# A hybrid decoder block on one core: transposing moves from GpSimd's queue, a double block of gate and z, and a third seven-product pair in every second gate and up block

## The chip, the cores and the metric

One core of a Trainium2 chip runs the whole kernel. The metric is the device time of one execution in microseconds; lower is better.

## What is computed

The reference is one layer of a decoder (256 tokens, model width 2048, all float32), and this is its skeleton:

```python
h = rmsnorm(x, ln1_w)
q, k, v, u, z, xbc, dt_raw, gate_logits = split(h @ w_in)
att  = sink_window_attention(q, k, v, sink)
pool = multiscale_pool(u, pool_w, pool_scale)
ssm  = ssd_mixer(z, xbc, dt_raw, ...)     # y * silu(z), normed in 4 groups of 512
g = sigmoid(gate_logits)                  # 3 x 2048 columns
merged = g[0]*(att @ w_attn_br) + g[1]*(pool @ w_pool_br) + g[2]*(ssm @ w_ssm_br)
x = x + merged @ w_out
h2 = rmsnorm(x, ln2_w)
gate, up = split(h2 @ w_gate_up)          # 2 x 5632 columns
x = x + (silu(gate) * up) @ w_down
out = rmsnorm(x, final_w)
```

## The kernel before

**Products in three.** Each float32 operand is split into a rounded part `hi` (a ScalarE copy, line 142) and the rest `lo` (a VectorE subtraction, line 143). A product is three matmuls, hi·hi, hi·lo and lo·hi (lines 225 to 227, function `three`). The activations stand transposed in SBUF, 128 of the inner dimension per tile ("k tile"); weights stream from HBM through the SyncE (SP) queue. `weights` loads into `raw` (3 buffers) and splits into two pieces of 128x1024, `whi` and `wlo`, of which there are 5 buffers each. So VectorE and ScalarE prepare weights at most five pieces ahead of TensorE.

**Blocks.** `tokens_block` makes 512 output columns for both token tiles. `two_blocks` makes 2 x 512 columns and takes the k tiles in pairs. A plain pair costs 8 products of 128x512 (24 matmuls, two weight pieces). A "seven" pair is a 2x2 by 2x2 block product by the Strassen and Winograd scheme: 7 products (21 matmuls). It needs sums of weights, made on VectorE from the tile `sraw` (1 buffer) and `vu` (1 buffer) in `block_weights` (lines 290 to 313: three splits of 128x1024, one addition of 128x1024, two additions of 128x512, one split of 128x512 into `shi`, `slo`), and sums of activations, made once in `block_forms` (tile `forms`). In a block of 8 pairs, pairs 0 and 1 are seven pairs and the order is 0, 2, 3, 4, 1, 5, 6, 7. Four of the eight accumulators (`tr`, `sm` in PSUM) end with the last seven pair and are folded into others by VectorE (lines 360 to 364).

**Turning.** A block of results [tokens x 512 columns] that becomes the next matmul's operand is transposed by `turn`: `move` issues 16 DMAs of 32x(2x128) blocks from SBUF to the tile `mid` (line 497), then `parts` transposes 32x32 squares on VectorE (line 502) and splits. There are four such turns for the SSD output (`ssm`, after each z group), four for the merged sum (`mp`), four for the residual (`x2p`) and eleven for the feed-forward (`f`). Before the change the `mp` moves go through GpSimd's (POOL) queue, all others through SP's queue, between the weight loads.

**Order.** `later` puts such side work in a list of tasks with a cost; `side`, called after each weight piece, adds a credit (1.4 for a piece of a `tokens_block`, 1.26 in `two_blocks`) up to 4, and takes one task when the credit is above zero. `pause` is a task that only costs: 5 after a move on SP, 12 after one on POOL. `need` takes tasks until the k tiles asked for are there. A scheduler then orders each engine's instructions from this program order.

**Stages around the change.** Gates of the pool branch and `branch(1, j)`; the z blocks with their norm (lines 1014 to 1030); `two_gates(2, 0)`, `two_branches(0)`, `two_gates(2, 2)`, `two_branches(2)`; the output projection with `residual`; eleven gate and up blocks in three parts with the down projection after each part; last, the final norm for each token tile (`rsqrt`, lines 457 to 467, called at 1158).

Of the kernel before, what the change touches and what calls it, by code (L numbers as in the profile page):

```python
# [16 lines left out]
P = 128  # L17
# [54 lines left out]
def hybrid_block(ctx: ExitStack, tc: tile.TileContext, ins, out):  # L72
# [181 lines left out]
    def block_forms(a, pairs):  # L254

        out = {}

        def forms_of(p):
            y = k2([2, T, P], F32, "fy")
            for k in range(2):  # L260
                dve.tensor_tensor(
                    y[:, k].rearrange("p t s -> p (t s)"),
                    a.hi(2 * p + k).bitcast(F32), a.lo(2 * p + k).bitcast(F32), ALU.add,
                )
            f = k2([4, P], F32, "ff4")
            dve.tensor_tensor(f[:, 1], y[:, 0, 1], y[:, 1, 1], ALU.subtract)
            dve.tensor_tensor(f[:, 2], f[:, 1], y[:, 0, 0], ALU.subtract)
            dve.tensor_tensor(f[:, 0], f[:, 2], y[:, 1, 0], ALU.add)
            dve.tensor_tensor(f[:, 3], y[:, 0, 0], y[:, 0, 1], ALU.subtract)
            t = late.tile([P, 2, 4, P], F32R, tag="forms", name="forms", bufs=4)  # L270
            split(f, t[:, 0], t[:, 1])
            out[p] = t

        for p in pairs:
            later(lambda p=p: forms_of(p), 3.0)
        return out
# [12 lines left out]
    def block_weights(loads):  # L289

        raw = late.tile([P, 4, NB], F32, tag="sraw", name="sraw", bufs=1)
        for to, src in loads:
            sp.dma_start(to(raw), src)
        vu = late.tile([P, 2, NB], F32, tag="vu", name="vu", bufs=1)
        out = []

        def part(src):
            hi = wpool.tile([P, 2, NB], F32R, tag="whi", name="whi", bufs=5)
            lo = wpool.tile([P, 2, NB], F32R, tag="wlo", name="wlo", bufs=5)
            split(src, hi, lo)  # L300
            out.extend((hi[:, i], lo[:, i]) for i in range(2))

        part(raw[:, 0:2])
        dve.tensor_tensor(vu, raw[:, 0::3], raw[:, 2:3].broadcast_to([P, 2, NB]), ALU.add)
        part(vu)
        dve.tensor_tensor(raw[:, 2], vu[:, 0], raw[:, 3], ALU.add)
        dve.tensor_tensor(raw[:, 0], raw[:, 2], raw[:, 1], ALU.add)
        part(raw[:, 0::2])
        hi = late.tile([P, NB], F32R, tag="shi", name="shi", bufs=2)
        lo = late.tile([P, NB], F32R, tag="slo", name="slo", bufs=2)  # L310
        split(raw[:, 3], hi, lo)
        out.append((hi, lo))
        return out

    def two_blocks(a, forms, w, k0, cols, nk, moved=True):

        if forms is None:
            q2, q4, q3, q8 = tr(), tr(), sm(), sm()  # L320
            seven, s1, u2, u3, s5 = [], None, None, None, None
        else:
            q1, q7, q5, q6 = tr(), tr(), sm(), sm()
            q2, q4, q3, q8 = acc(), acc(), acc(), acc()
            seven = [0, 1]
        plain = list(range(len(seven), nk // 2))
        share = len(plain) // max(len(seven), 1)
        order = [] if seven else plain
        for i, p in enumerate(seven):
            order += [p] + plain[i * share:(i + 1) * share]  # L330
        for p in order:
            ka, kb = 2 * p, 2 * p + 1
            a.need(ka)
            if p in seven:
                while p not in forms:
                    tasks.popleft()[0]()
                f = forms[p]
# [149 lines left out]
    def turn(block, k0, dst, scale=None, queue=sp):  # L487
# [24 lines left out]
            dst.waiting.discard(k0 // 4)  # L512

        later(move)
        pause(5.0 if queue is sp else 12.0)
        later(parts, 3.8)


# [400 lines left out]
    def two_gates(br, j):  # L919

        c0 = C_G + br * D + j * NB
        out = []
        for sums in two_blocks(h, h_forms, w_in, 0, (c0, c0 + NB), KD, False):
            sg = k4([T, NB], F32, "sg")
            for t, (q, more) in enumerate(sums):
                dve.tensor_tensor(more, q, more, ALU.add)
                act.activation(sg[:, t, :], more, AF.Sigmoid, scale=rstd1[:, t:t + 1])
            out.append(sg)
        return out

    def branch(br, j, a_parts, w, sg, banks=None):
        if br == 0:
# [8 lines left out]

    def two_branches(j, sgs):

        for n, sums in enumerate(two_blocks(ssm, s_forms, ins["w_ssm_br"][0], 0, (j * NB, (j + 1) * NB), KD)):
# [63 lines left out]
    sgs = two_gates(1, 1)  # L1008
    branch(1, 1, po, ins["w_pool_br"][0], sgs[0], [tr(), tr()])
    branch(1, 2, po, ins["w_pool_br"][0], sgs[1], [sm(), sm()])  # L1010
    branch(1, 3, po, ins["w_pool_br"][0], gate(1, 3))


    ssg = tiny([T, GROUPS], "ssg", 1)
    ssm = Parts(KD, "ssm")
    for g in range(GROUPS):
        for t, a in enumerate(tokens_block(h, KD, plain_loads(w_in, 0, C_Z + g * NB, NB), NB)):
            sz = k2([NB], F32, "sz")
# [5 lines left out]
        def finish(g=g):  # L1024
            rstd = rsqrt(ssg[:, :, g], NB, [T], "rsg")
            for t in range(T):
                dve.tensor_scalar(ys[g][:, t, :], ys[g][:, t, :], rstd[:, t:t + 1], None, ALU.mult)

        later(finish, 1.5)
        turn(ys[g], 4 * g, ssm, lambda k: norms[:, 0, k:k + 1])  # L1030

        if g == 0:
            s_forms = block_forms(ssm, (0, 1))

    sgs = two_gates(2, 0)
    finish_tasks()
# [14 lines left out]
        x2.append(xj)  # L1051
    ss2 = tiny([T, 4], "ss2", 1)
    x2p = Parts(KD, "x2p")
    forms = []

    def residual(j, accs):
        for t, a in enumerate(accs):
            dve.tensor_tensor(x2[j][:, t, :], a, x2[j][:, t, :], ALU.add)
            junk = k2([NB], F32, "junk")
            act.activation(junk, x2[j][:, t, :], AF.Square, accum_out=ss2[:, t, j:j + 1])  # L1060
        turn(x2[j], 4 * j, x2p, lambda k: norms[:, 1, k:k + 1])
        if j == 0:
            forms.append(block_forms(x2p, (0, 1)))

    w_out = ins["w_out"][0]
    for n, sums in enumerate(two_blocks(mp, None, w_out, 0, (0, NB), KD)):
# [12 lines left out]
    def down(j, c0, cols, i, accs):  # L1079

        for t, a in enumerate(accs):
            x_ = x2[j][:, t, c0:c0 + cols]
            dve.tensor_tensor(x_, a[:, :cols], x_, ALU.add)
            if i is not None:
                junk = k2([cols], F32, "junk")
                act.activation(junk, x_, AF.Square, accum_out=ss3[:, t, i:i + 1])
                for c in range(c0, c0 + cols, 256):
                    dve.tensor_tensor(
                        x2[j][:, t, c:c + 256], x2[j][:, t, c:c + 256], fw[(j * NB + c) // 256], ALU.mult
                    )  # L1090

    for some in FF_PARTS:
        f = Parts(4 * len(some), "f")
        for i, b in enumerate(some):
            a_ = k4([T, NB], F32, "ff")
            gates, ups = two_blocks(x2p, forms[0], wgu, 0, (b * NB, DFF + b * NB), KD)
            for t, (q, more) in enumerate(gates):
                dve.tensor_tensor(more, q, more, ALU.add)
                act.activation(a_[:, t, :], more, AF.Silu, scale=rstd2[:, t:t + 1])
# [20 lines left out]
                )  # L1120
                fw.extend(fw4[:, c, :] for c in range(4))
        for j in (0,) if last else (0, 2):
            sums = two_blocks(f, f_forms, wd, k0, (j * NB, (j + 1) * NB), nk)
# [19 lines left out]
    part = tiny([T], "part", 1)  # L1143
    dve.tensor_reduce(part, ss3, AX.X, ALU.add)
    dve.tensor_scalar(part, part, 1.0 / D, EPS, ALU.mult, ALU.add)
    out_v = out[0].rearrange("(t p) c -> p t c", p=P)
    for t in range(T):
        tok = slice(t * P, (t + 1) * P)
# [47 lines left out]
```

## Time and profile before

| what | us |
|---|---|
| median of 3 runs | 1646.37 |
| the runs | 1646.34, 1646.37, 1649.3 |
| the profiled execution: its own time | 1648.74 |
| its span in the trace | 1646.6 |
| granted TensorE clock, mean over the span | 0.998 |

The span is first to last instruction in the trace; 2.1 us of the execution's own time lie around it. TensorE is named PE, VectorE DVE, ScalarE ACT, GpSimd POOL, SyncE SP; a q behind the name means the engine's sequencer, which issues DMAs.

### The profile page before, as it was taken

Reading aid. Unit: us, or ns where it says so; the run is one execution under the profiler, and the core shown is the slowest. Engines: PE = TensorE matmul, PEld = TensorE weight load, DVE = VectorE, ACT = ScalarE, POOL = GpSimd, SP = SyncE. Lnnn points to the kernel's source line nnn. Section 1 sums busy time; section 2 is a strip of 40 time slices with the busy share of each in tenths; the row PEclk is TensorE's granted clock in tenths of the full one; section 3 lists DMA queues with packets and bytes.
Section 4 is the critical chain, followed back from the end, with each engine's and each line's share of the span. In section 5 each row is a group of like instructions: output and inputs, shape, how many; then the busy total and the mean of one; then the engine's idle time right before and its main releaser. Section 6 shows DMA issues by size and latency. Waiting matters only on the chain.

```text
span 1646.6 us, 20971 instructions
## 1 busy us (share of the span) xinstructions
PE 1626.4 (99%) x7689; PEld 1349.5 (82%) x7689; DVE 1318.8 (80%) x1738; ACT 898.2 (55%) x1190; POOL 96.8 (6%) x126
## 2 busy tenths in 40 slices
PE   8999999999999999999999999999999999999998
PEld 7888888888888888778888878888888888888887
DVE  5789898964786557688886799988879888888986
ACT  5467678644554457554545565554445555445553
POOL 1000001210220100002230000000000000000000
PEclk9999999999999999999999999999999999999999
DMA  8654566546566556566866666666666666666663
GB/s 250 204 159 146 166 196 205 179 158 200 161 224 212 197 185 212 155 233 203 265 221 191 202 211 226 206 215 215 204 205 193 219 214 217 205 203 199 216 212 103
DMA packets 214088, 328.83 MB, mean 200 GB/s; under 512 B 16253, under 2 KB 86145, under 8 KB 213985
## 3 DMA queue, kind: packets, MB, share of 16 engines
q1 hardware_dynamic: 209056, 317.77, 59.2%
q0 software_dynamic: 4176, 8.86, 1.9%
q8 instruction: 60, 0.98, 0.2%
q10 hardware_dynamic: 752, 0.86, 0.2%
q14 instruction: 44, 0.35, 0.1%
HBM read 313.25 MB, written 2.13 MB: 192 GB/s over the span
## 4 chain that ended last, share of the span: by engine, by line
PE 86%; SPq 4%; DMA 4%; DVE 3%; issue 1%; ACT 1%; DVEq 0%; ACTq 0%
PE acc L225 19%; PE acc L227 19%; PE acc L226 19%; PE acc L383 9%; PE acc L384 4%; SPq L497 4%; PE sm L226 2%; PE tr L227 2%; PE tr L226 2%; PE tr L225 2%; PE sm L225 2%; PE sm L227 2%; DVE wlo L143 1%; DMA raw<-in_w_gate_up_dram 1%; PE sm L868 1%
## 5 line engine op out<-in xcount | busy, mean ns | idle before, releaser
L143 DVE TENSOR_TENSOR wlo<-raw,whi 128x1024 fp32r<-128x1024 f32 (+2 forms) x500 | 600.2, 1215 | 155.8 <-ACT whi L142 154.7
L142 ACT CAST whi<-raw 128x1024 fp32r<-128x1024 f32 (+2 forms) x500 | 509.1, 1035 | 361.9 <-PE acc L227 244.3
L383 PE MATMUL acc<-h,whi 128*128 128x512 f32 x640 | 228.4, 400 | 0.0
L226 PE MATMUL acc<-wlo,x2p_hi 128*128 128x512 f32 x572 | 223.2, 390 | 1.2 <-DVE wlo L143 1.2
L225 PE MATMUL acc<-whi,x2p_hi 128*128 128x512 f32 x572 | 223.3, 390 | 0.0
L227 PE MATMUL acc<-whi,x2p_lo 128*128 128x512 f32 x572 | 223.0, 390 | 0.0
L226 PE MATMUL acc<-wlo,h 128*128 128x512 f32 (+1 forms) x508 | 195.5, 386 | 5.8 <-DVE wlo L143 5.7
L225 PE MATMUL acc<-whi,h 128*128 128x512 f32 (+1 forms) x508 | 196.9, 390 | 2.3 <-ACT whi L142 1.9
L227 PE MATMUL acc<-whi,h 128*128 128x512 f32 (+1 forms) x508 | 194.6, 386 | 0.0
L384 PE MATMUL acc<-h,wlo 128*128 128x256 f32 x640 | 180.3, 282 | 0.0
L142 ACT CAST whi<-sraw 128x1024 fp32r<-128x1024 f32 x84 | 88.1, 1049 | 121.8 <-PE acc L227 96.1
L383 PEld LDWEIGHTS acc<-h,whi 128*128 128x128 f32 x640 | 120.2, 188 | 30.1 <-issue 1.5
L143 DVE TENSOR_TENSOR wlo<-sraw,whi 128x1024 fp32r<-128x1024 f32 x84 | 102.6, 1221 | 45.4 <-ACT whi L142 45.2
L226 PEld LDWEIGHTS acc<-wlo,x2p_hi 128*128 128x128 f32 x572 | 107.4, 188 | 25.0 <-DVE wlo L143 2.3
L227 PEld LDWEIGHTS acc<-whi,x2p_lo 128*128 128x128 f32 x572 | 107.4, 188 | 23.0
L225 PEld LDWEIGHTS acc<-whi,x2p_hi 128*128 128x128 f32 x572 | 107.3, 188 | 23.0
L384 PEld LDWEIGHTS acc<-h,wlo 128*128 128x128 f32 x640 | 120.8, 189 | 1.8 <-issue 1.8
L226 PEld LDWEIGHTS acc<-wlo,h 128*128 128x128 f32 x508 | 95.8, 189 | 26.4 <-DVE wlo L143 7.2
L225 PEld LDWEIGHTS acc<-whi,h 128*128 128x128 f32 x508 | 95.6, 189 | 23.0 <-ACT whi L142 2.1
L227 PEld LDWEIGHTS acc<-whi,h 128*128 128x128 f32 x508 | 95.2, 188 | 19.4
L225 PE MATMUL acc<-whi,f_hi 128*128 128x512 f32 x244 | 95.3, 391 | 0.0
L227 PE MATMUL acc<-whi,f_lo 128*128 128x512 f32 x244 | 95.1, 390 | 0.0
(364 smaller groups left out, 2635.1 us busy)
## 6 DMA issues: line engine op xcount, KB each, us to landing
raw<-in_w_in_dram SPq DMA_DIRECT2D x80, 1024.0 KB, 5.3
raw<-in_w_gate_up_dram SPq DMA_DIRECT2D x132, 512.0 KB, 4.8
raw<-in_w_down_dram SPq DMA_DIRECT2D x62, 512.0 KB, 5.0
sraw<-in_w_gate_up_dram SPq DMA_DIRECT2D x44, 512.0 KB, 4.6
raw<-in_w_in_dram SPq DMA_DIRECT2D x43, 512.0 KB, 4.7
raw<-in_w_ssm_br_dram SPq DMA_DIRECT2D x24, 512.0 KB, 5.6
sraw<-in_w_down_dram SPq DMA_DIRECT2D x20, 512.0 KB, 5.0
raw<-in_w_attn_br_dram SPq DMA_DIRECT2D x8, 1024.0 KB, 5.1
```

The lines of the kernel that those rows point to most:

```text
L142: a = act.copy(hi, src)
L143: b = dve.tensor_tensor(lo, src, hi.bitcast(F32), ALU.subtract)
L225: pe.matmul(o, lhsT=xh, rhs=yh, start=first, stop=False)
L226: pe.matmul(o, lhsT=xh, rhs=yl, start=False, stop=False)
L227: pe.matmul(o, lhsT=xl, rhs=yh, start=False, stop=last)
L383: pe.matmul(accs[c], lhsT=hi[:, j, cols], rhs=a.both(k), start=k == 0, stop=False)
L384: pe.matmul(accs[c][:, :SEQ], lhsT=lo[:, j, cols], rhs=a.hi(k), start=False, stop=k == KD - 1)
L497: queue.dma_start(mid[32 * j:32 * j + 32, i], block[32 * i:32 * i + 32, :, j * P:(j + 1) * P])
L868: pe.matmul(p[:, i * HD:(i + 1) * HD], lhsT=mt[:, i, :], rhs=xdt[:, i, :], start=True, stop=True)
```

## The change

1. `turn` of the `ssm` groups and of the residual issues its 16 DMAs from POOL's queue in place of SP's; the pause after a move on POOL becomes 7 in place of 12, for the `mp` turns too.
2. The last gate block of the pool branch and the first z block become one `two_blocks` call with two seven pairs; its sums of z are passed through SiLU in place (`gated`), and `branch(1, 3)` comes behind it and accumulates in the `tr` banks.
3. Gate and up blocks 1, 3, 5, 7 and 9 take three of their eight pairs as seven pairs, in the order 0, 3, 4, 1, 5, 6, 2, 7. This needs one more `forms` tile (5 buffers, not 4); `shi` and `slo` go from 2 buffers to 1.
4. In the last norm the division and the constant go into the square root's scale and bias, and the Newton step is written with two VectorE operations in a row behind the reciprocal in place of three; the half that it needs is made beside the square root.

```diff
-            t = late.tile([P, 2, 4, P], F32R, tag="forms", name="forms", bufs=4)
+            t = late.tile([P, 2, 4, P], F32R, tag="forms", name="forms", bufs=5)
-        hi = late.tile([P, NB], F32R, tag="shi", name="shi", bufs=2)
-        lo = late.tile([P, NB], F32R, tag="slo", name="slo", bufs=2)
+        hi = late.tile([P, NB], F32R, tag="shi", name="shi", bufs=1)
+        lo = late.tile([P, NB], F32R, tag="slo", name="slo", bufs=1)
-    def two_blocks(a, forms, w, k0, cols, nk, moved=True):
+    def two_blocks(a, forms, w, k0, cols, nk, moved=True, seven=(0, 1)):
...
         for i, p in enumerate(seven):
-            order += [p] + plain[i * share:(i + 1) * share]
+            n = -(-len(left) // (len(seven) - i))
+            order += [p] + left[:n]
+            del left[:n]
...
-        pause(5.0 if queue is sp else 12.0)
+        pause(5.0 if queue is sp else 7.0)
...
-    branch(1, 3, po, ins["w_pool_br"][0], gate(1, 3))
...
-        turn(ys[g], 4 * g, ssm, lambda k: norms[:, 0, k:k + 1])
+        turn(ys[g], 4 * g, ssm, lambda k: norms[:, 0, k:k + 1], pool)
...
+    both = two_blocks(h, (h_forms,), w_in, 0, (C_G + D + 3 * NB, C_Z), KD, False)
+    sg = gate_of(both[0])
+    for q, more in both[1]:
+        dve.tensor_tensor(more, q, more, ALU.add)
+    gated(0, [more for _, more in both[1]], True)
+    branch(1, 3, po, ins["w_pool_br"][0], sg, [tr(), tr()])
+    for g in range(1, GROUPS):
+        gated(g, tokens_block(h, KD, plain_loads(w_in, 0, C_Z + g * NB, NB), NB))
...
-        turn(x2[j], 4 * j, x2p, lambda k: norms[:, 1, k:k + 1])
+        turn(x2[j], 4 * j, x2p, lambda k: norms[:, 1, k:k + 1], pool)
         if j == 0:
             forms.append(block_forms(x2p, (0, 1)))
+        if j == 1:
+            more_forms.append(block_forms(x2p, (2,)))
...
-            gates, ups = two_blocks(x2p, forms[0], wgu, 0, (b * NB, DFF + b * NB), KD)
+            gates, ups = two_blocks(
+                x2p, x_forms(), wgu, 0, (b * NB, DFF + b * NB), KD, True, (0, 1, 2) if b % 2 else (0, 1)
+            )
...
-        rstd = rsqrt(ss, D, [1], "rs3", part[:, t:t + 1])
+        rstd, more = tiny([1], "rs3_r"), part[:, t:t + 1]
+        act.activation(rstd, ss, AF.Sqrt, scale=1.0 / D, bias=more)
+        half, q = tiny([1], "rs3_v"), tiny([1], "rs3_q")
+        dve.tensor_scalar(half, ss, -0.5 / D, halves[:, t:t + 1], ALU.mult, ALU.add)
+        dve.reciprocal(rstd, rstd)
+        dve.scalar_tensor_tensor(q, rstd, half, rstd, ALU.mult, ALU.mult)
+        dve.scalar_tensor_tensor(rstd, q, 1.5, rstd, ALU.add, ALU.mult)
```

## Rows read from the trace of the kernel before

**Rows 1.** The page's first part: busy time, share of the span, instructions of each engine.

```profile
PE 1626.4 (99%) x7689; PEld 1349.5 (82%) x7689; DVE 1318.8 (80%) x1738; ACT 898.2 (55%) x1190; POOL 96.8 (6%) x126
```

**Rows 2.** The page's chain that ended last, shares of the span by line.

```profile
PE acc L225 19%; PE acc L227 19%; PE acc L226 19%; PE acc L383 9%; PE acc L384 4%; SPq L497 4%; PE sm L226 2%; PE tr L227 2%; PE tr L226 2%; PE tr L225 2%; PE sm L225 2%; PE sm L227 2%; DVE wlo L143 1%; DMA raw<-in_w_gate_up_dram 1%; PE sm L868 1%
```

**Rows 3.** Windows: length; PE, PEld, DVE, ACT, POOL busy; PE clock; DMA.

```profile
620.00:700.00 80.00, 78.16 (x344) 64.11 (x343) 60.16 (x93) 52.94 (x73) 0.00 (x0) 1.00 0.59 187
700.00:720.00 20.00, 16.13 (x64) 12.82 (x63) 19.04 (x25) 10.65 (x15) 0.00 (x0) 0.91 0.66 234
...
940.00:965.00 25.00, 23.79 (x102) 18.46 (x101) 24.17 (x35) 16.42 (x23) 0.00 (x0) 1.00 0.80 274
965.00:1600.00 635.00, 635.00 (x2781) 521.70 (x2780) 552.12 (x627) 332.41 (x358) 0.00 (x0) 1.00 0.63 208
```

**Rows 4.** Timeline of PE around 681 and 706 us: start, length, instruction, idle before.

```profile
681.24 0.50 PE L226 MATMUL acc<-wlo,h 128*128 128x512 f32 x1 [1.84 <-DVE wlo L143]
...
706.68 0.50 PE L226 MATMUL acc<-wlo,h 128*128 128x512 f32 x1 [3.87 <-DVE wlo L143]
...
708.14 0.63 PE L225 MATMUL acc<-whi,h 128*128 128x512 f32 x1
...
710.70 0.59 PE L225 MATMUL acc<-whi,h 128*128 128x512 f32 x1
711.12 0.39 PE L226 MATMUL acc<-wlo,h 128*128 128x512 f32 x1
```

**Rows 5.** Timeline of SP's queue, 640 to 720 us.

```profile
659.82 10.77 SPq L497 DMA_DIRECT2D mid<-y  x16
...
671.83 0.93 SPq L293 DMA_DIRECT2D sraw<-in_w_in_dram  x2
...
686.42 11.50 SPq L497 DMA_DIRECT2D mid<-y  x16
```

**Rows 6.** Timeline of DVE, 678 to 710 us.

```profile
678.76 1.23 DVE L304 TENSOR_TENSOR vu<-sraw 128x1024 f32<-128x1024 f32 x1 [0.56 <-DMA sraw<-in_w_in_dram]
...
699.49 1.09 DVE L502 STREAM_TRANSPOSE tt<-mid 128x512 f32<-128x512 f32 x1 [4.88 <-DMA mid<-y]
...
705.40 4.62 DVE L143 TENSOR_TENSOR wlo<-raw,whi 128x1024 fp32r<-128x1024 f32 x4
```

**Rows 7.** Waits of PE's weight loads, 620 to 1620 us: total, times, longest.

```profile
PEld acc L226 <- DVE wlo L143: 8.8, 5, 4.3
```

**Rows 8.** `mp` moves on POOL, transposes behind them; issues (min/median/max).

```profile
847.89 8.51 POOL L497 DMA_DIRECT2D mid<-m  x16 [41.94 <-ACT whi L142]
857.15 0.54 POOL L497 DMA_DIRECT2D mid<-m  x1 [0.74 <-issue]
...
861.65 2.06 DVE L502 STREAM_TRANSPOSE tt<-mid 128x512 f32<-128x512 f32 x2 [4.41 <-DMA mid<-m]
873.36 2.06 DVE L502 STREAM_TRANSPOSE tt<-mid 128x512 f32<-128x512 f32 x2 [2.48 <-DMA mid<-m]
...
L497 POOL DMA_DIRECT2D mid<-m x64: 539/539/597, 766.2 to 867.9; - x64
```

**Rows 9.** Windows of gate and up blocks 7 and 9; DVE's additions.

```profile
1318.20:1360.69 42.49, 42.49 (x188) 34.91 (x187) 36.36 (x40) 22.40 (x24) 0.00 (x0) 1.00 0.62 210
1488.17:1530.67 42.50, 42.50 (x188) 34.92 (x187) 39.59 (x54) 23.21 (x26) 0.00 (x0) 1.00 0.62 201
...
L304 DVE TENSOR_TENSOR vu<-sraw 128x1024 f32<-128x1024 f32 x42 | 52.3, 1246 | 3.5 <-DMA sraw<-in_w_ssm_br_dram 1.6 <-DMA sraw<-in_w_gate_up_dram 1.3 <-DMA sraw<-in_w_in_dram 0.6
L306 DVE TENSOR_TENSOR sraw<-vu,sraw 128x512 f32<-128x512 f32 x42 | 28.8, 685 | 0.0
```

**Rows 10.** Timeline of DVE in the last norm, second token tile.

```profile
1639.48 0.21 DVE L461 TENSOR_SCALAR rs_v<-ss_last,part 128x1 f32<-128x1 f32 x1
...
1640.36 0.16 DVE L465 TENSOR_TENSOR rs_q<-rs_q,rs_v 128x1 f32<-128x1 f32 x1
1640.55 0.16 DVE L466 SCALAR_TENSOR_TENSOR rs_r<-rs_q,rs_r 128x1 f32<-128x1 f32 x1
```

More of the change, by code (lines that the diff above doesn't have):

```diff
@@ L324, in two_blocks @@
             q2, q4, q3, q8 = acc(), acc(), acc(), acc()
-            seven = [0, 1]
         plain = list(range(len(seven), nk // 2))
-        share = len(plain) // max(len(seven), 1)
         order = [] if seven else plain
+        left = list(plain)
         for i, p in enumerate(seven):
-            order += [p] + plain[i * share:(i + 1) * share]
+            n = -(-len(left) // (len(seven) - i))
+            order += [p] + left[:n]
+            del left[:n]
         for p in order:
@@ L334, in two_blocks @@
             if p in seven:
-                while p not in forms:
+                while not any(p in part for part in forms):
                     tasks.popleft()[0]()
-                f = forms[p]
+                f = next(part[p] for part in forms if p in part)
                 b11, b21, v, u, z, w_, b22 = block_weights(block_loads(w, k0 + ka, cols, moved))
@@ L921, in two_gates, with gate_of @@
         c0 = C_G + br * D + j * NB
[L922 to L929, printed above, removed]
+        return [gate_of(sums) for sums in two_blocks(h, (h_forms,), w_in, 0, (c0, c0 + NB), KD, False)]
+    def gate_of(sums):
+        sg = k4([T, NB], F32, "sg")
+        for t, (q, more) in enumerate(sums):
+            dve.tensor_tensor(more, q, more, ALU.add)
+            act.activation(sg[:, t, :], more, AF.Sigmoid, scale=rstd1[:, t:t + 1])
+        return sg
     def branch(br, j, a_parts, w, sg, banks=None):
@@ L942, in two_branches @@
     def two_branches(j, sgs):
-        for n, sums in enumerate(two_blocks(ssm, s_forms, ins["w_ssm_br"][0], 0, (j * NB, (j + 1) * NB), KD)):
+        for n, sums in enumerate(two_blocks(ssm, (s_forms[0],), ins["w_ssm_br"][0], 0, (j * NB, (j + 1) * NB), KD)):
             for t, (q, more) in enumerate(sums):
@@ L1010, in hybrid_block, with gated @@
     branch(1, 2, po, ins["w_pool_br"][0], sgs[1], [sm(), sm()])
-    branch(1, 3, po, ins["w_pool_br"][0], gate(1, 3))
     ssg = tiny([T, GROUPS], "ssg", 1)
     ssm = Parts(KD, "ssm")
-    for g in range(GROUPS):
-        for t, a in enumerate(tokens_block(h, KD, plain_loads(w_in, 0, C_Z + g * NB, NB), NB)):
-            sz = k2([NB], F32, "sz")
+    s_forms = []
+    def gated(g, accs, in_place=False):
+        for t, a in enumerate(accs):
+            sz = a if in_place else k2([NB], F32, "sz")
             act.activation(sz, a, AF.Silu, scale=rstd1[:, t:t + 1])
@@ L1022, in hybrid_block, with finish @@
             act.activation(junk, ys[g][:, t, :], AF.Square, accum_out=ssg[:, t, g:g + 1])
-        def finish(g=g):
+        def finish():
             rstd = rsqrt(ssg[:, :, g], NB, [T], "rsg")
@@ L1029, in hybrid_block @@
         later(finish, 1.5)
-        turn(ys[g], 4 * g, ssm, lambda k: norms[:, 0, k:k + 1])
+        turn(ys[g], 4 * g, ssm, lambda k: norms[:, 0, k:k + 1], pool)
         if g == 0:
-            s_forms = block_forms(ssm, (0, 1))
+            s_forms.append(block_forms(ssm, (0, 1)))
+    both = two_blocks(h, (h_forms,), w_in, 0, (C_G + D + 3 * NB, C_Z), KD, False)
+    sg = gate_of(both[0])
+    for q, more in both[1]:
+        dve.tensor_tensor(more, q, more, ALU.add)
+    gated(0, [more for _, more in both[1]], True)
+    branch(1, 3, po, ins["w_pool_br"][0], sg, [tr(), tr()])
+    for g in range(1, GROUPS):
+        gated(g, tokens_block(h, KD, plain_loads(w_in, 0, C_Z + g * NB, NB), NB))
     sgs = two_gates(2, 0)
@@ L1053, in hybrid_block @@
     x2p = Parts(KD, "x2p")
-    forms = []
+    forms, more_forms = [], []
     def residual(j, accs):
@@ L1090, in down, with x_forms @@
                     )
+    def x_forms():
+        return (forms[0], more_forms[0])
     for some in FF_PARTS:
@@ L1122, in hybrid_block @@
         for j in (0,) if last else (0, 2):
-            sums = two_blocks(f, f_forms, wd, k0, (j * NB, (j + 1) * NB), nk)
+            sums = two_blocks(f, (f_forms,), wd, k0, (j * NB, (j + 1) * NB), nk)
             for n in range(2):
@@ L1145, in hybrid_block @@
     dve.tensor_scalar(part, part, 1.0 / D, EPS, ALU.mult, ALU.add)
+    halves = tiny([T], "halves", 1)
+    dve.tensor_scalar(halves, part, -0.5, None, ALU.mult)
     out_v = out[0].rearrange("(t p) c -> p t c", p=P)
```

## The prediction

> **What bounds the kernel now.** I read the page's busy times first: PE is busy 99% of the span, DVE 80%, POOL 6% [rows 1]. So a removed matmul is worth its own time wherever PE never waits, and POOL has room for more. The chain says the same with one exception: nearly all of it is matmul lines, but 4% is SPq L497, SP issuing the small moves of `turn` [rows 2]. That is the line which the change takes from SP for eight of its nineteen turns, so I asked where PE stands still. The windows answer it: from 965 to 1600 us PE is busy without a gap, while from 620 to 700 it lacks 1.84 us, from 700 to 720 it lacks 3.87 us, from 940 to 965 it lacks 1.21 us [rows 3]. From 620 to 1620 us the weight loads of PE wait five times for a `wlo`, 8.8 us in all [rows 7]. These few places are all there is to win by better timing; all else must come from fewer matmuls.
>
> What the two large gaps hang on is seen by setting SP's queue beside DVE. SP issues 16 moves for a z group from 659.82 to 670.6; only then, at 671.83, come the loads of `sraw` [rows 5], which DVE takes up at 678.76 after having waited for them [rows 6], and PE waits until 681.24 [rows 4]. The next 16 moves hold SP from 686.42 to 697.9 [rows 5]. DVE stands at a transpose for 4.88 us, waiting for their data, to 699.49, and makes four weight pieces in a row only from 705.40 [rows 6]; PE waits until 706.68 [rows 4]. Behind that wait the granted clock is down, 0.91 over 20 us [rows 3]: the matmuls from 708.14 to 710.70 come every 0.427 us, for a short time the lower of the clock's two levels (1.2 GHz), and at 711.12 it is the upper one again [rows 4].
>
> **Moves from POOL's queue.** What goes from SP is 8 x 16 issues, some 10.8 to 11.5 us for a turn [rows 5]; the weight loads no longer stand behind them. On POOL an issue takes 0.54 us, the same at the minimum and the median of 64 [rows 8]. From the first issue to the transpose that waited for the data is 13.8 us (847.89 to 861.65) and 16.2 us (857.15 to 873.36) [rows 8]; on SP it was 686.42 to 699.49, 13.1 us [rows 5, 6], so POOL lands 0.7 to 3.1 us later. Against that stands the pause of 7 where SP's turns had 5: with a credit of 1.4 for each weight piece, two more credits are wanted before the transposes, so they come one to two pieces later in the program. A piece is 12 matmuls, 2.7 us, so 2.7 to 5.5 us: about the later landing or more. The `mp` turns get a pause of 7 for 12; their data was ready long before for the first two, and for the last two `need` fetches the transposes whatever the pause is, so I count nothing. What is queued behind a transpose that comes too early is the split of the next weight pieces on DVE, and PE waits for those; the cover is the five pieces of lead. On POOL itself, only additions into `m4` stand behind the moves, and nothing reads those before `two_branches(2)`.
>
> The price. If both gaps go: 1.84 + 3.87 us [rows 3], and the slow clock behind the second, 8 matmuls that took 0.427 in place of 0.23, 1.6 us [rows 4]. Sum 7.3 us. The bound below is nothing won (DVE waits for POOL as it did for SP), and a loss is a rival. I take 6.9, since the gaps follow SP's moves step by step. At the residual the gap is 1.2 us [rows 3], but DVE is busy there for 24.17 of 25 us, and the change adds a third set of `forms` just before; the loads come earlier, the work does not get less. Between 0 and 1.2 I take 0.7.
>
> A rule that speaks against this part. The row: 64 issues on POOL took 539 ns at minimum and median, 597 at most, with DVE at work all around [rows 8]. The Trainium skill (SBUF — State Buffer, "Who interferes with whom") says that a DMA issued from GpSimd has its descriptors written by GpSimd, that VectorE in a two-port mode locks it out of the port for this, and advises the SP or ACT queue. By the row the moves cost what is counted above; by the rule, taken widely, they would be stretched, and the gain of 6.9 us would be gone, which is the last rival below. So far the trace does not agree: no issue is longer than 597 ns.
>
> **Gate and z as a double block.** Two blocks of 96 matmuls become one of 2 x 21 + 6 x 24 = 186. A gate and up block of 186 takes 42.50 us where PE has no gap [rows 9], so 0.2285 us for each, and 6 fewer are 1.37 us. The extra work on DVE is hidden by its idle time; without that cover it would be some 8 us (2 x 4.1, worked out in the next part). The block needs the `sm` banks soon after `branch(1, 2)` has filled them: a stall of up to 1 us is possible. I take 1.37.
>
> **A third seven pair in five blocks.** 15 matmuls fewer: 3.43 us. DVE gains work: a plain pair is two splits, a seven pair three, one addition of the same size, and three of half of it. Back to back a split takes 1.155 us (4.62 for four [rows 6]), and the half ones by their 0.685 against 1.246 [rows 9] some 0.6. So a block adds 1.155 + 1.155 + 3 x 0.6 = 4.1 us. The blocks of odd number have DVE at 39.59 us (1, 5 and 9, in which `forms` of the next product are made too) or 36.36 us (3 and 7) [rows 9]. With 4.1 more they have 43.7 and 40.5, for a PE time of 42.5 - 0.7 = 41.8. So in three blocks DVE has 1.9 us too much to do, and lives on the lead that it brings along. There is a second tight place: the last seven pair is now followed by one plain pair before the next block's first. `sraw` has one buffer, and from load to first use were 6.9 us (671.83 to 678.76 [rows 5, 6]), then some 6.4 us of DVE work until the last large piece is split, 13.3 in all. PE gives 21 + 24 matmuls, 10.3 us, and 2 us more until it wants that piece. So if the load starts no sooner than the seven pair itself, 1 us is lacking. Bounds of the loss: nothing (lead covers it), or 3 x 1.9 + 2 x 1.0 = 7.7 us. I take 1.5, near the low end, since PE has no gap at all from 965 to 1600 us now [rows 3]. Net 1.9 us.
>
> **The last norm.** Off the chain go one operation before the root (0.21 us and the step to the next) and one behind it (0.2 us from 1640.36 to 1640.55 [rows 10]): 0.45 us for the second token tile, with which the kernel ends. The one new operation stands beside the root.
>
> **Sum.** 6.9 + 0.7 + 1.37 + 1.9 + 0.45 = 11.3 us. From the profiled execution's own 1648.74 (span 1646.6 and 2.1 around it) that makes 1637.4. That execution stands 2.4 us above the median, near the highest of the three runs; from the median, 1646.37, the same sum gives **1635.1 us**. All at their best: 7.3 + 1.2 + 1.37 + 3.43 + 0.45 = 13.8, so 1632.6.
>
> **Rivals.**
> *DVE becomes the bound in the odd blocks* (loss 7.7 rather than 1.5). For it: 43.7 us of work in 41.8. Against: the blocks between leave it 4 us and more. Sum 11.3 - 6.2 = 5.1: 1641.3.
> *The gaps stay though SP is free*, because DVE has the splits, sums and transposes of two stages at once there. For it: DVE is busy 19.04 of 20 us behind the wait [rows 3]. Against: it stood idle for 4.88 us just before [rows 6]. Sum 11.3 - 6.9 - 0.7 = 3.7: 1642.7.
> *Slower: DVE stands at the transposes until POOL's moves have landed.* Place: the eight moved turns. If the scheduler leaves the transposes where they are in DVE's order, each waits 0.7 to 3.1 us longer than now; four of them (the last two z groups, the last two of the residual) come where DVE has no lead left. It decides from a lateness that uses up the 6.9 us won and the 4.4 of the other parts, 2.8 us for each of the four. At 3.1 each, with the gaps of now kept and 1.6 us of slow clock behind each new one, it is 12.4 + 6.4 - 3.7 = 15 us more: 1661; with two turns hit and not four, 1652.
> *Moves stretched by DVE*, as a mechanism of its own: if an issue took twice its 0.54 us, a move would land 8.6 us later, four turns would lose some 5.5 us each beyond the 3.1, and the time would be above 1670. Against it stand the 64 equal issues [rows 8].
>
> **Chances.** Forecast 0.58, 1632 to 1638. DVE the bound 0.15. Gaps stay 0.11. Transposes wait 0.13. Stretched moves 0.03. Range 1631 to 1644: it reaches over the first two rivals and leaves out the rest. A measurement of this kernel can tell about 0.2%, 3.3 us, from no change; 1643.1 is the line. Faster: 0.58, 0.13 of the first rival, 0.05 of the second: 0.76. Same: the rest of these two with a little of the third: 0.10. Slower: 0.14.
>
> **What would show it.** Right: no L497 on SP between 600 and 960 us; PE without the waits of 1.84 and 3.87 us and at full clock there; 186 matmuls for gate and z; 183 in odd blocks, 41.8 us each with no wait for `wlo`. Wrong: DVE waiting at L502 for `mid` for several us with a gap on PE behind it; waits of PE for `wlo` at the first seven pair behind each odd block; POOL issues well over 0.54 us.

## The result, and the profile after

The changed kernel takes **1685.74 us** (median of 4 runs, 1683.44 to 1690.5); the kernel before, in the same comparison, 1646.85. The ratio is 1.0237 (95% interval 1.0211 to 1.0263): 39 us slower, where 11.3 us faster was predicted. The profiled execution has 1687.01 us, a span of 1685.0 and a mean granted clock of 0.987, against 0.998 before.

The page's first part:

```profile
PE 1638.2 (97%) x7668; PEld 1352.1 (80%) x7668; DVE 1352.6 (80%) x1787; ACT 909.0 (54%) x1206; POOL 164.3 (10%) x254
```

There are 21 matmuls fewer than in [rows 1], the 6 and 15 that the change removes. Yet PE's busy time is 11.8 us longer: a matmul at the lower clock counts as busy for longer. The chain that ended last is followed back here only to about 611 us, so its shares can't be set beside [rows 2]. Where the time went, the windows tell (columns as in [rows 3]):

```profile
620.00:700.00 80.00, 74.79 (x317) 60.80 (x316) 58.67 (x89) 51.29 (x70) 25.55 (x48) 0.96 0.63 199
700.00:720.00 20.00, 18.74 (x83) 15.15 (x82) 14.23 (x19) 7.39 (x11) 0.06 (x1) 1.00 0.51 162
...
965.00:1600.00 635.00, 611.69 (x2614) 497.07 (x2613) 539.60 (x617) 319.88 (x346) 0.00 (x0) 0.98 0.59 197
```

Of 965 to 1600 us read the count. Where PE is solid, [rows 3] have 2781 matmuls in these 635 us, 0.2283 us each; now there are 2614. 167 fewer, times 0.2283, are 38 us lost, standstills and slow clock together. Of these, 23.3 us are standstills (635.00 less 611.69); the rest is matmuls at the lower clock. Most of the loss is here, in the feed-forward. In front of it, the gap of 3.87 us after 700 has shrunk to 1.26, but the one before 700 has grown from 1.84 to 5.21, with the clock at 0.96, and four small ones stand behind 720 (2.43 us in sum). From 620 to 965 us PE has 1447 matmuls, before the change 1472: 25 fewer, 5.7 us. From 940 to 965 us PE is busy all 25 us; in [rows 3] it lacked 1.21.

**An odd feed-forward block's end.** The timeline of DVE in the changed kernel from 1549 us, as PE (at 1550.06) comes to the third seven pair of block 9, and behind it single rows of SP's queue, of ACT and of PE. Block 10 begins on PE at 1560.39.

```profile
1549.91 1.23 DVE L143 TENSOR_TENSOR wlo<-sraw,whi 128x1024 fp32r<-128x1024 f32 x1 [1.19 <-ACT whi L142]
1551.05 2.36 DVE L143 TENSOR_TENSOR wlo<-raw,whi 128x1024 fp32r<-128x1024 f32 x2
1553.32 0.69 DVE L362 TENSOR_TENSOR u<-sm,s 128x512 f32<-128x512 f32 x1
1556.39 1.23 DVE L143 TENSOR_TENSOR wlo<-sraw,whi 128x1024 fp32r<-128x1024 f32 x1 [2.39 <-ACT whi L142]
1557.54 0.68 DVE L363 TENSOR_TENSOR u<-tr,u 128x512 f32<-128x512 f32 x1
...
1560.40 0.68 DVE L1117 TENSOR_TENSOR s<-acc,s 128x512 f32<-128x512 f32 x1
...
1562.00 0.68 DVE L1124 TENSOR_TENSOR s<-acc,s 128x512 f32<-128x512 f32 x1
1562.61 1.21 DVE L304 TENSOR_TENSOR vu<-sraw 128x1024 f32<-128x1024 f32 x1
...
1570.45 1.23 DVE L143 TENSOR_TENSOR wlo<-sraw,whi 128x1024 fp32r<-128x1024 f32 x1 [1.17 <-ACT whi L142]
```
```profile
1551.16 0.88 SPq L293 DMA_DIRECT2D sraw<-in_w_gate_up_dram  x2
```
```profile
1555.31 1.05 ACT L142 CAST whi<-sraw 128x1024 fp32r<-128x1024 f32 x1 [3.05 <-DMA sraw<-in_w_gate_up_dram]
```
```profile
1564.95 0.80 PE L225 MATMUL tr<-whi,forms 128*128 128x512 f32 x1 [2.83 <-ACT whi L142]
...
1566.87 0.79 PE L226 MATMUL tr<-wlo,forms 128*128 128x512 f32 x1 [0.70 <-DVE wlo L143]
...
1570.47 0.80 PE L225 MATMUL sm<-whi,forms 128*128 128x512 f32 x1 [1.53 <-ACT whi L142]
1571.07 0.63 PE L225 MATMUL acc<-whi,x2p_hi 128*128 128x512 f32 x1
1571.49 0.63 PE L225 MATMUL acc<-shi,forms 128*128 128x512 f32 x1
```

The last split of the block's third seven pair (1549.91) frees `sraw`, and at once, at 1551.16, the next block's load is issued. ACT, which waited 3.05 us for it, takes it up at 1555.31; DVE stands 2.39 us until 1556.39, though the folding of the block's end is still to come. From then DVE has work without a pause: the first split, the folding of the block that ends, its sums, the `forms` of the next product. The addition that makes `vu` comes only at 1562.61, 7.3 us after ACT had the data; the last large piece is split at 1570.45. PE stands 2.83, 0.70 and 1.53 us, and the matmuls at 1571 come every 0.42 us (the lower of the two levels, 1.2 GHz), until 1574.

In the kernel before, at the end of the same block, SP's load and DVE's last large split of the next block's first seven pair:

```profile
1509.29 0.88 SPq L293 DMA_DIRECT2D sraw<-in_w_gate_up_dram  x2
```
```profile
1528.24 1.23 DVE L143 TENSOR_TENSOR wlo<-sraw,whi 128x1024 fp32r<-128x1024 f32 x1 [0.59 <-ACT whi L142]
```

That is 18.95 us, and 19.29 after the change (1551.16 to 1570.45): the stretch is hardly longer than it was. But the load stood 21.4 us ahead of the next block (1530.66), and now stands 9.2 us ahead of it.

The ends of blocks 3 and 7 starve PE as well:

```profile
1126.86 0.67 PE L225 MATMUL sm<-whi,forms 128*128 128x512 f32 x1 [3.95 <-ACT whi L142]
```
```profile
1392.40 0.50 PE L225 MATMUL sm<-whi,forms 128*128 128x512 f32 x1 [2.69 <-ACT whi L142]
```

It is not that DVE has more work than the block has time: while PE makes block 3 (1078.08 to 1119.94 us) DVE is busy 34.60 of the 41.86 us, and in block 9 (1518.53 to 1560.39) 35.58 of 41.86.

**The z groups.** The same kernel from 600 to 730 us: DVE's transposes, then single rows of PE, SP's queue and POOL.

```profile
615.51 2.06 DVE L503 STREAM_TRANSPOSE tt<-mid 128x512 f32<-128x512 f32 x2 [5.62 <-DMA mid<-y]
648.68 2.05 DVE L503 STREAM_TRANSPOSE tt<-mid 128x512 f32<-128x512 f32 x2 [5.69 <-DMA mid<-y]
674.74 2.04 DVE L503 STREAM_TRANSPOSE tt<-mid 128x512 f32<-128x512 f32 x2 [6.99 <-DMA mid<-y]
705.77 1.08 DVE L503 STREAM_TRANSPOSE tt<-mid 128x512 f32<-128x512 f32 x1 [6.58 <-DMA mid<-y]
```
```profile
677.94 0.80 PE L226 MATMUL acc<-wlo,h 128*128 128x512 f32 x1 [5.06 <-DVE wlo L143]
```
```profile
667.78 0.88 SPq L293 DMA_DIRECT2D sraw<-in_w_in_dram  x2
```
```profile
662.91 5.86 POOL L498 DMA_DIRECT2D mid<-y  x11 [16.70 <-ACT whi L142]
669.73 2.67 POOL L498 DMA_DIRECT2D mid<-y  x5 [0.95 <-DMA mid<-y]
689.91 4.26 POOL L498 DMA_DIRECT2D mid<-y  x8 [17.52 <-DVE y L1030]
695.80 4.26 POOL L498 DMA_DIRECT2D mid<-y  x8 [1.62 <-DMA mid<-y]
```

SP is free, and its load of `sraw` is issued at 667.78, 4 us sooner than in [rows 5]. It helps little: DVE stands at the transpose from 667.75 to 674.74, and PE waits 5.06 us for the split behind it. The four waits are 24.88 us in sum. In the kernel before the same four were 11.1 us, of which [rows 6] show the longest, 4.88. Its waits of DVE from 600 to 760 us, and the third of the four:

```profile
DVE tt L502 <- DMA mid<-y: 11.1, 4, 4.9
```
```profile
672.25 2.06 DVE L502 STREAM_TRANSPOSE tt<-mid 128x512 f32<-128x512 f32 x2 [3.76 <-DMA mid<-y]
```

In the last norm, second token tile, DVE has 1.09 us from the reading of the accumulator (1678.04) to the use of the root (1679.13); before, 1.38 (1639.36 to 1640.74).

### The profile page after: what moved, and what is told of

It reads as the page before. It is cut to its first block, busy times and chain, and to the rows that moved or that the text cites. A ratio compares the mean times of both kernels' runs of the same rounds, so it can differ in the third digit from the quotient of the medians.

```text
span 1685.0 us, 21059 instructions
## 1 busy us (share of the span) xinstructions
PE 1638.2 (97%) x7668; PEld 1352.1 (80%) x7668; DVE 1352.6 (80%) x1787; ACT 909.0 (54%) x1206; POOL 164.3 (10%) x254
## 4 chain that ended last, share of the span: by engine, by line
PE 40%; DVE 10%; DMA 5%; SPq 3%; issue 2%; ACT 2%; POOL 1%; DVEq 0%; ACTq 0%
PE acc L226 11%; PE acc L225 11%; PE acc L227 11%; DVE wlo L143 4%; SPq L498 3%; DMA mid<-y 2%; DMA sraw<-in_w_gate_up_dram 1%; ACT whi L142 1%; PE sm L225 1%; PE tr L227 1%; PE sm L226 1%; PE sm L227 1%; PE tr L226 1%; PE tr L225 1%; POOL mid L498 1%
## 5 line engine op out<-in xcount | busy, mean ns | idle before, releaser
L143 DVE TENSOR_TENSOR wlo<-raw,whi 128x1024 fp32r<-128x1024 f32 (+2 forms) x486 | 579.4, 1210 | 123.7 <-ACT whi L142 122.1
L142 ACT CAST whi<-raw 128x1024 fp32r<-128x1024 f32 (+2 forms) x486 | 493.9, 1034 | 311.7 <-PE acc L227 207.2
L225 PE MATMUL acc<-whi,x2p_hi 128*128 128x512 f32 x542 | 213.2, 393 | 0.7 <-DVE s L1117 0.7
L226 PE MATMUL acc<-wlo,x2p_hi 128*128 128x512 f32 x542 | 212.4, 392 | 0.0
L227 PE MATMUL acc<-whi,x2p_lo 128*128 128x512 f32 x542 | 212.1, 391 | 0.0
L142 ACT CAST whi<-sraw 128x1024 fp32r<-128x1024 f32 x98 | 102.9, 1050 | 172.6 <-DVE sraw L307 70.7
L225 PE MATMUL acc<-whi,h 128*128 128x512 f32 (+1 forms) x496 | 192.1, 390 | 0.7 <-ACT whi L142 0.3
L227 PE MATMUL acc<-whi,h 128*128 128x512 f32 (+1 forms) x496 | 190.3, 386 | 0.0
L143 DVE TENSOR_TENSOR wlo<-sraw,whi 128x1024 fp32r<-128x1024 f32 x98 | 120.0, 1225 | 68.3 <-ACT whi L142 67.9
L225 PEld LDWEIGHTS acc<-whi,x2p_hi 128*128 128x128 f32 x542 | 102.9, 190 | 23.3 <-DVE s L1117 1.4
L227 PEld LDWEIGHTS acc<-whi,x2p_lo 128*128 128x128 f32 x542 | 102.4, 189 | 21.7
L225 PEld LDWEIGHTS acc<-whi,h 128*128 128x128 f32 x496 | 93.5, 189 | 20.7 <-ACT h L145 1.1
L226 PE MATMUL acc<-wlo,f_hi 128*128 128x512 f32 x244 | 95.4, 391 | 0.0
```

The source lines that it names most:

```text
L142: a = act.copy(hi, src)
L143: b = dve.tensor_tensor(lo, src, hi.bitcast(F32), ALU.subtract)
L225: pe.matmul(o, lhsT=xh, rhs=yh, start=first, stop=False)
L226: pe.matmul(o, lhsT=xh, rhs=yl, start=False, stop=False)
L227: pe.matmul(o, lhsT=xl, rhs=yh, start=False, stop=last)
```

## The experiments

Theory: two causes, each on its own. A, the third seven pair starves PE behind every odd block; B, the transposes of the moved turns come too early, and DVE stands at them. Within A, two things were to be told apart, the one `sraw` buffer and DVE's work at the block's end; within B, DVE's wait and SP's time. Times are medians; the kernel before had 1646.5 to 1647.8 beside them.

**The third pair left out of the change** (e1).

```diff
-                x2p, x_forms(), wgu, 0, (b * NB, DFF + b * NB), KD, True, (0, 1, 2) if b % 2 else (0, 1)
+                x2p, x_forms(), wgu, 0, (b * NB, DFF + b * NB), KD, True, (0, 1)
```

> The changed kernel with two seven pairs in every gate and up block, all else as changed. In the changed kernel PE stands still or runs slowly for about 38.8 us at the ends of the five odd blocks. Theory A (the third pair makes all of that): 1685.7 - 38.8 + 3.4 for the 15 matmuls that come back = 1650, no PE wait behind 980 us. Rival (the moves on POOL's queue delay the feed-forward stage too): 1670 or more, with waits left behind 980 us.

Measured: 1649.97 us, ratio 1.0021 (1.0012 to 1.0030). PE is busy for all of 965 to 1600 us, with 2786 matmuls. So the third pair costs 35.8 us net of the 15 matmuls that it saves, and the rest of the change is still about 3.5 us slower than before.

**The eight moved turns back on SP's queue**, pauses 5 and 12 as before, with the third pair (e2) and without (e3).

```diff
-        turn(ys[g], 4 * g, ssm, lambda k: norms[:, 0, k:k + 1], pool)
+        turn(ys[g], 4 * g, ssm, lambda k: norms[:, 0, k:k + 1])
...
-        pause(5.0 if queue is sp else 7.0)
+        pause(5.0 if queue is sp else 12.0)
```

> The changed kernel with the eight moves back on SP's queue and the pauses of 5 and 12; the third pair stays. Theory A (POOL moves cost some 6 us in the z groups and 2 us at the output projection, give 2 us back at the residual): 1685.7 - 6 = 1679 to 1680. Rival (POOL moves are behind most of the loss): 1650 or less.

> The changed kernel with two seven pairs in every block and the eight moves back on SP's queue (pauses 5 and 12): what is left of the change is the double block of gate and z and the last norm. Theory D (what costs time around the moves is VectorE standing at the transposes until the data are there, on either queue): 1646.5 - 1.8 for the work saved, and 0 to 3 more for longer waits, 1645 to 1648. Rival (as the prediction had it: a move on SP holds up the weight loads, and that is what PE waits for): 7 us above the same kernel with POOL moves (1650), 1657.

Measured: e2 1685.83 us, 1.0243 (1.0226 to 1.0260); e3 1650.63 us, 1.0019 (1.0010 to 1.0027). Each equals its partner on POOL, though both were expected to be faster: which of the two queues takes all the moves, each with its pauses, makes no difference. With the moves on SP the third pair costs 35.2 us, so A doesn't hang on B.

**The seven pairs one plain pair apart, early in the odd block** (e4): order 0, 3, 1, 4, 2, 5, 6, 7, so that three plain pairs follow the last.

> The changed kernel with the odd blocks in the order 0, 3, 1, 4, 2, 5, 6, 7, so that three plain pairs stand behind the last seven pair and not one; as many matmuls, as much VectorE work. Theory B (the loss comes from the last seven pair standing close before the next block's first, with one sraw buffer and the folding of the accumulators between): most of the 38.8 us comes back, 1650 to 1656. Rival (VectorE has more to do in an odd block than PE has time): 43.7 us of work in 41.8 in any order, so the loss stays, 1675 or more.

Measured: 1686.76 us, 1.0245 (1.0229 to 1.0260). That is the rival's time, but the place has changed. Behind blocks 3 and 7 PE no longer waits; it waits inside the odd blocks, in block 1 at 1002.69 and 1006.16 us, at the third seven pair, which now stands one plain pair behind the second. That agrees with the theory that one plain pair is too little between two seven pairs, wherever they stand. But behind blocks 1, 5 and 9 some 3.2 us of standing stay even with three plain pairs between (behind block 1: 1.40 at 1032.62 and 1.76 at 1035.58). There DVE also makes the `forms` of the next product, so the distance is not the whole cause.

**A weight buffer for the next seven pair** (e5): the seven pairs' weights come from the pool of `raw`, with 4 buffers shared by all pairs in place of 3 and 1. To make room `k2` has 5 buffers in place of 6, here and in e10 to e12.

```diff
-        raw = late.tile([P, 4, NB], F32, tag="sraw", name="sraw", bufs=1)
+        raw = wpool.tile([P, 4, NB], F32, tag="raw", name="sraw", bufs=4)
```

> The changed kernel with the weights of seven pairs taken from the same pool as the others, four buffers in place of three and one (k2 has 5 buffers in place of 6 to make room), so that the loads of the next block's first seven pair need not wait for the last one's splits. Theory C (the single sraw buffer is what makes the next seven pair late): 20 us or more come back, 1650 to 1665. Rival (VectorE's folding and splits in the 10 us between the two pairs are too much, whenever the data come): 1678 or more.

Measured: 1664.02 us, 1.0109 (1.0093 to 1.0125), 21.7 us back. Not all of it in the feed-forward: from 965 to 1600 us PE has 2689 matmuls, 75 more than in the changed kernel (17 us), and from 620 to 965 us 1479 against 1447, 32 more (7 us).

**DVE doesn't wait for the moves.** The transposes of the z groups and of the residual read the block itself, not `mid`, without the third pair; moves on POOL (e6) or, with the pauses of before, on SP (e7). The moves are still issued, but their data are not used. `direct` is true for these eight turns.

```diff
-                    mid[:, :, t].rearrange("p i (c k) -> p i k c", k=4),
+                    block[:, t].rearrange("p (i c k) -> p i k c", i=4, k=4) if direct else mid[:, :, t].rearrange("p i (c k) -> p i k c", k=4),
```

> Two seven pairs everywhere, moves on POOL's queue as in the changed kernel; but the transposes of the z and residual turns read the block before the move, so VectorE does not wait for those eight moves (they are still issued; the output is not the reference's). Theory D: PE's waits between 600 and 960 us are gone, 1650 - 12 = 1637 to 1640. Rival (VectorE has too much to do there in any case): 1645 or more.

> The same with the moves on SP's queue: VectorE does not wait for the eight moves, but SP still issues them between the weight loads (the output is not the reference's). Theory D: as fast as the POOL version without the wait, 1637 to 1640. Rival (SP's time is a second cause of its own): 4 us or more above it, with waits of PE for wlo left behind late loads.

Measured: e6 1635.45 us, 0.9923 (0.9908 to 0.9939), e7 1639.13 us, 0.9947 (0.9934 to 0.9961). With the transposes' wait gone, 14.5 us come back against e1, more than the 3.5 that e1 is slower than before: the kernel before waits there too. One wait of DVE for these moves is left in each, behind the last z group: 4.24 us in e6, and in e7 5.09, until 695.77. SP's time is a cause of its own in at most the difference, 3.7 us: in e7 PE still lacks 2.49 us of 620 to 700, until 698.63, and that comes behind DVE's wait. The windows of e6:

```profile
620.00:700.00 80.00, 80.00 (x354) 66.06 (x353) 62.20 (x86) 55.73 (x75) 25.53 (x48) 1.00 0.63 205
700.00:720.00 20.00, 20.00 (x90) 16.45 (x89) 18.31 (x21) 12.66 (x15) 0.00 (x0) 1.00 0.56 192
```

**Each move over two queues** (e8), without the third pair: 8 of the 16 DMAs of every turn that had POOL's queue go through SP's.

```diff
-                    queue.dma_start(mid[32 * j:32 * j + 32, i], block[32 * i:32 * i + 32, :, j * P:(j + 1) * P])
+                    q_ = (sp, pool)[j % 2] if queue is pool else sp
+                    q_.dma_start(mid[32 * j:32 * j + 32, i], block[32 * i:32 * i + 32, :, j * P:(j + 1) * P])
```

> Two seven pairs everywhere; each of the twelve moves that POOL has in the changed kernel is split, eight issues on SP and eight on POOL. Theory D: a move takes some 9 us in place of 14, VectorE's waits of 6 us shrink to 1 to 3, 1650 - 8 = 1642, range 1639 to 1646. Rival (the order on VectorE follows the planner's idea of the landing, and transposes move forward as much as the data): no gain, 1649 to 1651.

Measured: **1635.04 us, 0.9921 (0.9907 to 0.9934)**, better than expected, and the best kernel here. Its transposes that wait (the first z group's doesn't), then a row of POOL and one of SP:

```profile
640.77 2.05 DVE L504 STREAM_TRANSPOSE tt<-mid 128x512 f32<-128x512 f32 x2 [3.42 <-DMA mid<-y]
662.16 2.05 DVE L504 STREAM_TRANSPOSE tt<-mid 128x512 f32<-128x512 f32 x2 [2.31 <-DMA mid<-y]
688.76 2.09 DVE L504 STREAM_TRANSPOSE tt<-mid 128x512 f32<-128x512 f32 x2 [2.39 <-DMA mid<-y]
```
```profile
682.39 4.25 POOL L499 DMA_DIRECT2D mid<-y  x8 [22.20 <-DMA raw<-in_w_in_dram]
```
```profile
682.12 5.08 SPq L499 DMA_DIRECT2D mid<-y  x8
```

From the first DMA to the transpose are 6.64 us (682.12 to 688.76), where POOL alone took 15.86 (689.91 to 705.77) and SP alone 13.1 [rows 5, 6]. DVE's waits sum to 8.1 us, and PE feels none of them: from 620 to 965 us PE is busy all 345 us, with 1518 matmuls against 1447 in the changed kernel.

**The third pair on top of the split moves** (e9); then with the shared buffers (e10); then with four additions of DVE left out as well (e11); the shared buffers alone, without the third pair, as the control (e12); and, last, the additions left out with the one `sraw` (e13). Left out in the odd blocks is the line that adds the two banks of a sum, four times 0.68 us (lines 1117 and 1124):

```diff
             for t, (q, more) in enumerate(gates):
-                dve.tensor_tensor(more, q, more, ALU.add)
+                if b % 2 == 0:
+                    dve.tensor_tensor(more, q, more, ALU.add)
```

> The changed kernel, third seven-product pair kept, but each move for the state-space norm and the residual shared half and half between SP's and GpSimd's queues, as in e8_split. If the two losses (the third pair in the feed-forward, the moves in front) add up independently, the median is that of e8_split plus what the third pair cost between e1_no_third and the changed kernel (1685.7 - 1650.0 = 35.8): 1671 (1668 to 1674), with TensorE's standstills at the ends of the odd feed-forward blocks as in the changed kernel (some 39 us with the slow clock behind them) and none of the z groups. If a late start of the feed-forward were part of the third pair's loss, less would be left of it, and the time would be under 1662.

> e9_split_third with the seven-product pairs' weights in a pool of four buffers shared with the plain pairs, so that the next pair's load need not wait for the split of the pair before. In e5_shared this gave back 21.7 us. If that adds to the split moves: 1635 + 14 = 1649 (1645 to 1653), with some 20 us of standstill and slow clock left at the ends of odd blocks. If the buffer alone were the cause: 1633 to 1636.

> e10_split_shared with the four additions left out that add the two banks of each gate and up sum in the five odd feed-forward blocks (so one bank of each sum is missing from the output). They take 4 x 0.68 = 2.7 us of VectorE in the stretch where it is solidly busy. If VectorE's work between the last seven-product pair and the next block's first is what is left of the loss, 2.7 us per block come back, and with them slow-clock stretches behind the standstills: 1635 to 1641. If something else sets the rest (the order of TensorE's products, the loads), it stays at e10_split_shared's time within 2 us.

> The control for both: e8_split (no third pair, moves shared between two queues) with the shared pool of four buffers. If sharing the buffers costs or gives nothing by itself: 1635 (1633 to 1637). If the plain pairs' loads are held up by the seven-product pairs' in the same pool, 1638 or more.

> e9_split_third (single weight buffer for the seven-product pairs) with only the four additions per odd block left out, as in e11_no_folds (one bank of each gate and up sum is missing from the output). e9 took 1666.2, the shared buffers alone (e10) 1656.9, both (e11) 1639.5, without the third pair 1635. If VectorE's work is the cause and the single buffer is held long only because VectorE splits late, leaving the folds out does most of it alone: 1642 to 1652. If the single buffer has a loss of its own, since its load can start only after the pair's own last split, the two add: 1666.2 less about 17 minus what only the buffer hides, and more than 9 us above e11, so 1649 or more. If the buffer rules alone: above 1658.

Measured:

| | us | ratio to before | matmuls 965 to 1600 us |
|---|---|---|---|
| e9, third pair, one `sraw` | 1666.17 | 1.0111 (1.0093 to 1.0129) | 2629 |
| e10, shared buffers | 1656.88 | 1.0058 (1.0040 to 1.0076) | 2682 |
| e13, no additions, one `sraw` | 1647.16 | 0.9997 (0.9987 to 1.0006) | 2719 |
| e11, both | 1639.47 | 0.9950 (0.9934 to 0.9966) | 2762 |
| e12, no third pair, shared | 1635.94 | 0.9929 (0.9913 to 0.9945) | 2786 |
| e8, no third pair | 1635.04 | 0.9921 (0.9907 to 0.9934) | 2786 |

With the moves out of the way the third pair costs 31.1 us (e9 less e8; 36 had been expected). Of these the buffer gives 9.3 back, the additions 19.0, both together 26.7: they nearly add up, and DVE's part is the larger. 14 us of DVE's work (5 x 4 x 0.68) are worth 19 us of time: by the windows below the standstills shrink by 11 us, from 20.7 to 9.7, and the rest is matmuls that are no longer slow. Behind block 9 the stretch from the load to the last large split shrinks by 2.94 us, 18.86 in e9 and 15.92 in e13, about what was left out there (2.7). The buffer alone isn't enough: in e10 that load is issued at 1511.51, long before it is wanted, and PE still stands 3.25 us, until 1539.77, for the splits behind the folding. e10 came out 8 us above its expectation, partly because some 7 of the 21.7 us that e5 had won lay ahead of the feed-forward. For e9 and then for e13, the window, SP's load and DVE's last large split:

```profile
965.00:1600.00 635.00, 614.34 (x2629) 500.54 (x2628) 542.22 (x618) 323.83 (x351) 0.00 (x0) 0.98 0.58 198
```
```profile
1532.83 0.88 SPq L293 DMA_DIRECT2D sraw<-in_w_gate_up_dram  x2
```
```profile
1551.69 1.23 DVE L143 TENSOR_TENSOR wlo<-sraw,whi 128x1024 fp32r<-128x1024 f32 x1 [1.17 <-ACT whi L142]
```
```profile
965.00:1600.00 635.00, 625.34 (x2719) 510.12 (x2719) 548.11 (x619) 335.14 (x363) 0.00 (x0) 1.00 0.61 204
```
```profile
1515.87 0.88 SPq L293 DMA_DIRECT2D sraw<-in_w_gate_up_dram  x2
```
```profile
1531.79 1.23 DVE L143 TENSOR_TENSOR wlo<-sraw,whi 128x1024 fp32r<-128x1024 f32 x1 [0.51 <-ACT whi L142]
```

Even e11 is 3.5 us above e12, although its third pair saves 15 matmuls: PE still lacks 3.4 us from 965 to 1600 us, in waits for splits of weights. What those last microseconds hang on stays open. Not tried, and so open, are the kernel before with nothing but the moves changed, and longer pauses on POOL.

## Why the prediction was wrong

**The third seven pair: the term that failed, by its size.** It stood with 3.43 us won and 1.5 lost, bound 7.7. The 15 matmuls did go, but the loss was 31 (e9) to 36 us (e1) net of them. The prediction had named both places, DVE's work in odd blocks and the one plain pair left between the last seven pair and the next block's first, and had even reckoned that a load can't start before the seven pair itself: right, it started at 1551.16, during it. Wrong was what follows. It counted 6.9 us from load to first use and 6.4 of work to the last large split, 13.3 in all, and so 1 us lacking. The trace has 11.45 us to the use that was meant, the addition that makes `vu` (1562.61), and 19.29 to the last large split (1570.45). The 6.9 us came from a row of the z groups; at the end of block 9 the kernel before already took 18.95 us for the same stretch, so a row of this stage would have warned of it, though there the stretch had time to be long. The work of the block's end had been counted in the block's total, 43.7 us, but not at its place: DVE does it just between the load and the splits that PE wants next, and e13 beside e9 shows that this work sets most of the standstill. Behind blocks 3 and 7, where the prediction saw no excess (40.5 in 41.8), PE stood 3.95 and 2.69 us too. And behind these standstills came stretches at the lower clock, which the prediction charged in front of the feed-forward and not here. The argument "PE has no gap at all from 965 to 1600 us" was no cover: in the kernel before, three plain pairs behind the last seven pair let the load and the splits go ahead of the next block; the change took two of these away. e4 gave them back at the price of the distance inside the block, and lost as much.

**The moves: the step that failed is that the pause of 7 puts the transposes one to two pieces later.** From DVE's rows, the large weight splits between the scaling of a block and its transpose were 5, 5, 5 and 5 before and 4, 5, 4 and 5 after: no transpose came later by a piece, two came one piece earlier. In time, DVE reached the four 7.1 us sooner behind the scaling, in sum, and the data landed 6.7 us later; that makes the difference between 11.1 and 24.88 us of waiting. Whether the program's order already had the transposes there or the scheduler put them forward, no run shows. It isn't POOL alone: with the moves back on SP (e3) the waits were still 17.2 us, so a part comes with the new order of the stage, and how large that part is by itself stays open. The freed SP did what was predicted, and it was worth at most the 3.7 us between e6 and e7, since DVE, in front of the loaded weights, stood at a transpose. The prediction had read the two gaps as following "SP's moves step by step"; e6 shows that they followed DVE's wait for the moved data, which is long on either queue. For the first gap the trace of before had it: DVE stood 3.76 us at a transpose, to 672.25, and then only 0.56 us for `sraw`, the wait that the prediction named. This is the third rival, at its place in the z groups but not at its price: e1, the change without the third pair, is 3.5 us slower than before, and the rival had 15 us for four turns, or 1652 us for two. At the residual it did not strike: DVE waits there for 7.9 us where it was 5.3, but PE's gap is gone, as predicted. The `mp` turns, put at nothing, cost PE 1.66 us behind 872 us (1.14 and 0.52); with the moves on SP and the pause of 12 (e3) that gap isn't there.

**What came true.** The 6 matmuls of gate and z, and the 15; the odd blocks themselves take 41.9 to 42.3 us, where 41.8 was predicted, and the loss stands behind them. PE waited at the first seven pair behind each odd block, which the prediction had named as a sign of being wrong. The last norm has 0.29 us less between the accumulator and the use of the root; 0.45 was predicted. The first rival (DVE the bound in odd blocks) had the right place and a fifth of the price, but by the amount of work, which the blocks' windows don't bear out. The fourth (stretched moves) has nothing for it in the issues: all 192 on POOL took 539 to 599 ns, median 542. So the rule of the Trainium skill (SBUF — State Buffer, "Who interferes with whom") was not seen at work in the changed kernel either. With both failures taken away, e8 is 12.5 us faster than the kernel before beside it (1647.5); the prediction's terms without the third pair sum to 9.4. That these are near each other is no proof of the terms, since e8 also splits the moves, those of the `mp` turns too.

## What to carry to other kernels

An engine's busy share in a block, even its sum against the block's length, doesn't tell whether a single buffer is filled in time: lay the instructions in their order between the moment that frees the buffer and the one that needs it, and count the work of the block's end among them. When an engine waits for a transfer, ask first whether the transfer can be made shorter (two queues) before asking whose queue it blocks. And a gap of PE can cost more than its length: count the slow matmuls behind it, at every place.

## What the runs showed of the hardware

Sixteen small SBUF moves on POOL's queue take longer than sixteen times the 0.54 us of an issue (8.6 us): in the move that began at 662.91, after 11 issues, and in that of 689.91, after 8, POOL waited 0.95 and 1.62 us for an older move of the same turn. By the table of transfers from 640 to 740 us a move took a median of 4.3 us to land there, and when each queue had 8 of them (600 to 740 us of e8) it was 1.9 us on POOL and 2.1 on SP:

```profile
mid<-y POOLq DMA_DIRECT2D x42, 32.0 KB, 4.3
```
```profile
mid<-y SPq DMA_DIRECT2D x32, 32.0 KB, 2.1
mid<-y POOLq DMA_DIRECT2D x32, 32.0 KB, 1.9
```

The number of moves on a queue doesn't explain it alone: sixteen `mid<-y` moves on SP landed in a median of 1.9 us in the kernel before, and in e8 the `mp` and residual moves, split in the same way, took 3.6 to 4.4 us on either queue (600 to 1000 us). What sets the landing, no run here shows.
